# An issue-order mark on the VectorE modulations of a two-layer hybrid trunk

## The chip, the cores and the metric

The kernel runs on one NeuronCore of one Trainium2 chip. The metric is the device time of one execution in microseconds (us); lower is better. Three executions of the kernel before are given, and one more was taken with the hardware profiler; all rows below are from that one.

## The reference

The reference is one inference step of a diffusion trunk of two layers over 128 context tokens and 128 latent tokens, with a model width of 2048, in float32. What matters here, per layer:

```python
mods = silu(cond) @ w_mod[l] + b_mod[l]          # split in six: shift1, scale1, gate1, shift2, scale2, gate2
h = rms_norm(x, norm1_g) * (1 + scale1) + shift1
x = x + gate1 * (mixers(h @ w_in) @ w_out)       # linear attention, softmax attention, DeltaNet
h = rms_norm(x, norm2_g) * (1 + scale2) + shift2
x = x + gate2 * (square(relu(h @ w_ff1)) @ w_ff2)   # 4 * 2048 wide
```

The six modulations are numbered m = 0 to 5 in that order, so (0, 5) is gate2 of layer 0. Each is a product of two condition vectors with a 2048 x 2048 matrix.

## The kernel before, in words

Both groups of tokens go through the layers together: x lies as 16 tiles of 128 features by 256 tokens. Weights come from HBM in halves of 128x1024 float32 (512 KB, tile `raw`, six buffers, issued on SP's queue). For each half, ScalarE rounds it to `hi` and VectorE forms the rest `lo` = raw - hi (`split_half`), three buffers each; TensorE then does 16 matmuls with `hi` (the rounded activations and their rest) and 8 with `lo`. One half takes TensorE some 2.8 us in the profile. A unit of 128 output features has two halves and then an evacuation: `res_evac` for w_out and w_ff2 (VectorE adds gate times product to `x`; after w_out, and in the last pass of layer 0, it also scales the new x for the next norm into `hid` or `act` and adds its square to `sqacc`), `ff_evac` for w_ff1 (relu, square and rest).

The stretch that the change touches lies in each layer between w_out and w_ff1. w_out has 32 halves. Then `norm_lead` normalises: `get_rstd` sums the squares on TensorE (`st`), a Newton iteration of small VectorE instructions (`nv`, `n2t`, `n2y`) gives the reciprocal root, `diag` and a matmul (`bcb`) spread it. Meanwhile `lead_gemm` runs the first six units of w_ff1 (12 halves, tiles `gl`, `gl2`) on x scaled but not yet divided by the norm, and corrects them afterwards (`ld`). Interleaved with it `normed` makes the 16 tiles of the true normalised input: two `ht` on VectorE, two `hu` and one rounding on ScalarE, one rest (`act<-hu,act`) on VectorE, for each k. All later units of w_ff1 need all 16. The same function runs at the start of layer 1 on w_in, and in layer 1 again before w_ff1. Then follow four passes of w_ff1 and four of w_ff2, 32 halves each, in the order ff1(0), ff1(1), ff2(0), ff1(2), ff2(1), ff1(3), ff2(2), ff2(3).

The modulations are made in three ways. Two are made at the start. Most are made on TensorE (`mod_pe`: 16 steps, each with two w_mod halves and a few matmuls into `mod`). Four, listed in ONDV as (0, 5), (1, 1), (1, 0) and (1, 5), are made on VectorE by `mod_dv`: a transposed half `mraw` (512 KB, three buffers, SP's queue) is multiplied with a condition vector `sb` and summed along the row in one instruction (`tensor_tensor_reduce`; the profile calls it CUSTOM_DVE_ANT_0, with output `junk`, and a short accumulator read stands behind it; the order prints both as ISA). A modulation has 64 of these, 16 feature tiles by two conditions by two halves of the sum, so 256 in all. Below, such an instruction is a MAC. The first half of the sum goes to `part`, the second to `modc`. `junk` has one buffer, so the MACs of the program stay in sequence.

The order on each engine is not that of the code. The program is written down in one order and a scheduler (`schedule_with_timeline_sim=True`) then sets a static order per engine from its own model, with the written order as priority. `start_mod(l, 5)` is called in `ff1(0)`, behind `norm_lead`, but nothing holds its instructions there: they need only their own loads. They have to be done before `ff2(0)` uses gate2. An instruction that waits holds back all that stands behind it on its engine.

Of the kernel before, what the change touches and what calls it, by code (L numbers as in the profile page):

```python
# [10 lines left out]
F32 = mybir.dt.float32  # L11
# [4 lines left out]
ALU = mybir.AluOpType  # L16
# [25 lines left out]
def tile_hybrid_step(ctx: ExitStack, tc: tile.TileContext, A: dict, O: dict):  # L42
# [17 lines left out]
    ve, se = Timed(nc.vector, 1 / 960, 0.13), Timed(nc.scalar, 1 / 1400, 0.27)  # L60
# [339 lines left out]
    def mod_dv(l, m, modc, bm):  # L400
        mac = X["mac"]
        part = mdp.tile([P, 16, 2], F32, tag="part", name="part")
        i = ONDV.index((l, m))
        order = [(half, n) for half in range(2) for n in range(16)]

        def fetch(u):
            raw = mac.tile([P, 1024], F32, tag="mraw", name="mraw", bufs=3)
            nc.sync.dma_start(raw, A["w_modT"][i, order[u][0], order[u][1]])
            return raw

        nxt = fetch(0)
        for u, (half, n) in enumerate(order):
            raw = nxt
            if n == 0:
                sb = mac.tile([P, 2, 1024], F32, tag="sb", name="sb")
                nc.gpsimd.dma_start(sb.rearrange("p c j -> p (c j)"), scd[half].partition_broadcast(P))
                yield
            nxt = fetch(u + 1) if u + 1 < len(order) else None
            for c in range(2):
                junk = mac.tile([P, 1024], BF16, tag="junk", name="junk")  # L420
                ve.tensor_tensor_reduce(
                    out=junk, in0=raw, in1=sb[:, c], scale=1.0,
                    scalar=part[:, n, c : c + 1] if half else bm[:, m, n : n + 1], op0=ALU.mult, op1=ALU.add,
                    accum_out=modc[:, m, n, c : c + 1] if half else part[:, n, c : c + 1],
                )
            yield

    def mod_pe(l, m, modc, bm):
# [65 lines left out]
    def normed(rstd, dst, scl, shf):  # L494
        for k in range(16):
            t = X["np"].tile([P, 256], F32, tag="ht", name="ht", bufs=2)
            u = X["np"].tile([P, 256], F32, tag="hu", name="hu", bufs=2)
            for g in range(2):
                s = slice(g * P, g * P + P)
                ve.scalar_tensor_tensor(t[:, s], X["x"][:, k, s], scl[:, k, g : g + 1], rstd[:, s], ALU.mult, ALU.mult)  # L500
                se.activation(u[:, s], t[:, s], AF.Identity, bias=shf[:, k, g : g + 1])
            se.activation(dst[:, k, 0:256], u, AF.Copy)
            ve.tensor_tensor(dst[:, k, 256:512], u, dst[:, k, 0:256].bitcast(F32), ALU.subtract)
            yield

    def norm_lead(srcs, xsp, dst, scl, shf, ldp, sink=None):
        se.activation(xsp[:, :, 256:258], shf, AF.Copy)
        ve.tensor_tensor(xsp[:, :, 514:516], shf, xsp[:, :, 256:258].bitcast(F32), ALU.subtract)
        rstd = get_rstd()
        return lead_gemm(srcs, xsp, rstd, normed(rstd, dst, scl, shf), ldp, sink)  # L510
# [132 lines left out]
    for l in range(L):  # L643
# [171 lines left out]
        else:  # L815
            nlead = list(zip(FIRST, first))
            for j in FIRST[len(first) : 13]:
                for _ in range(2):
                    if nlead:
                        u, ps = nlead.pop(0)  # L820
# [832 lines left out]
```

## Time and profile before

| | us |
|---|---|
| median of three executions | 2579.03 |
| lowest and highest | 2578.31 and 2583.78 |
| the profiled execution, its own time | 2589.99 |
| span of its trace | 2588.2 |
| TensorE busy (matmuls) | 2503.7, 97% of the span |
| VectorE busy | 1822.5, 70% |
| ScalarE busy | 1225.7, 47% |

The profiled execution is 11 us above the median. Matmuls are pipelined and their ends are modelled, so a busy TensorE is not one at its peak. The same work appears once per layer, so a stretch of layer 0 can be held against its counterpart in layer 1.

### The profile page before, as it was taken

What the parts mean: (1) busy time and instruction counts of PE and PEld (TensorE: products, weight loads), DVE (VectorE), ACT (ScalarE), POOL (GpSimd) and SP (SyncE); (2) the same over time, 40 slices, a digit from 0 to 9 for tenths busy, and PEclk for the clock granted to TensorE, in tenths of its full rate; (3) what the DMA queues carried; (4) which work ended last, traced back from release to release, by engine and by line L of the source; (5) the groups of instructions that cost most, each with busy time, mean ns of one, the idle gap of its engine ahead of it and who ended that gap; (6) DMA issues with size and microseconds to landing.
All of it is one profiled execution on the core that took longest, in us unless ns stands there. A gap on an engine that the chain in (4) does not pass through costs nothing.

```text
span 2588.2 us, 47588 instructions
## 1 busy us (share of the span) xinstructions
PE 2503.7 (97%) x18860; PEld 2250.6 (87%) x18860; DVE 1822.5 (70%) x3510; ACT 1225.7 (47%) x1977; POOL 31.2 (1%) x59
## 2 busy tenths in 40 slices
PE   6999999988799999999999999999999999999999
PEld 4777677778799999999999888898999989999888
DVE  3456767698998889988456767697764565564665
ACT  3356244434655345344344763455575435445433
POOL 1000000000000000000000000000000000000000
PEclk9999999998899999999999999999999999999999
DMA  9875767797799999998777765445556666666664
GB/s 362 313 253 180 274 213 279 274 371 247 241 327 340 326 336 326 333 333 294 235 235 237 245 232 172 141 134 166 176 182 185 185 190 188 185 192 187 185 199 141
DMA packets 171935, 622.00 MB, mean 240 GB/s; under 512 B 20496, under 2 KB 21072, under 8 KB 170688
## 3 DMA queue, kind: packets, MB, share of 16 engines
q1 hardware_dynamic: 165600, 600.12, 68.4%
q0 software_dynamic: 3712, 15.59, 1.7%
q8 instruction: 148, 2.42, 0.4%
q10 hardware_dynamic: 2400, 3.24, 0.4%
q14 instruction: 75, 0.61, 0.1%
HBM read 612.57 MB, written 6.31 MB: 239 GB/s over the span
## 4 chain that ended last, share of the span: by engine, by line
PE 89%; DMA 4%; DVE 3%; ACT 2%; issue 1%; SPq 0%; ACTq 0%; DVEq 0%
PE g L86 67%; PE gt L86 6%; PE mod L86 4%; PE gl L86 4%; DMA raw<-w_mod 2%; DMA raw<-w_tok 1%; DVE lo L56 1%; ACT hi L56 1%; PE ga L86 1%; DVE junk L56 1%; PE eb L86 1%; DMA raw<-w_in 1%; PE fb L86 0%; PE fbm L86 0%; PE ob L86 0%
## 5 line engine op out<-in xcount | busy, mean ns | idle before, releaser
L56 ACT ACTIVATE hi<-raw 128x1024 fp32r<-128x1024 f32 (+1 forms) x742 | 784.5, 1058 | 1104.2 <-PE g L86 791.3
L56 DVE TENSOR_TENSOR lo<-raw,hi 128x1024 fp32r<-128x1024 f32 (+1 forms) x742 | 905.1, 1220 | 431.9 <-ACT hi L56 416.4
L86 PE MATMUL g<-act,hi 128*128 128x256 f32 (+1 forms) x7488 | 1054.1, 291 | 23.9 <-ACT ffr L56 7.4
L86 PEld LDWEIGHTS g<-act,hi 128*128 128x128 f32 x7488 | 955.6, 189 | 100.5 <-ACT hi L56 27.4
L86 PE MATMUL g<-act,lo 128*128 128x256 f32 x4000 | 562.8, 282 | 3.2 <-DVE lo L56 3.2
L86 PEld LDWEIGHTS g<-act,lo 128*128 128x128 f32 x4000 | 516.8, 190 | 14.5 <-DVE lo L56 4.9
L56 DVE SCALAR_TENSOR_TENSOR x<-g,modc,x 128x128 f32<-128x128 f32 x448 | 142.3, 348 | 185.8 <-PE g L86 180.5
L86 PE MATMUL g<-hid,hi 128*128 128x256 f32 (+1 forms) x1536 | 261.3, 319 | 0.0
L86 PEld LDWEIGHTS g<-hid,hi 128*128 128x128 f32 x1536 | 217.1, 188 | 23.1 <-ACT hi L56 5.0
L86 PE MATMUL mod<-raw,sc 128*32 128x512 f32 (+1 forms) x1280 | 152.1, 537 | 28.9 <-DMA raw<-w_mod 25.3
L56 DVE CUSTOM_DVE_ANT_0 junk<-mraw,sb,bm 128x1024 bf16<-128x1024 f32 x128 | 164.0, 1282 | 5.3 <-DMA sb<-scd 2.5
L56 DVE CUSTOM_DVE_ANT_0 junk<-mraw,sb,part 128x1024 bf16<-128x1024 f32 x128 | 164.1, 1282 | 2.1 <-DMA sb<-scd 1.7
L86 PE MATMUL gt<-hi,act 128*128 128x512 f32 x512 | 144.5, 414 | 3.7 <-ACT hi L56 3.7
L86 PE MATMUL g<-hid,lo 128*128 128x256 f32 x1024 | 141.8, 281 | 0.0
L86 PEld LDWEIGHTS g<-hid,lo 128*128 128x128 f32 x1024 | 134.6, 188 | 5.4
L86 PEld LDWEIGHTS gt<-hi,act 128*128 128x128 f32 x512 | 94.6, 192 | 41.1 <-issue 13.7
L86 PEld LDWEIGHTS mod<-raw,sc 128*32 128x32 f32 x1280 | 30.1, 110 | 67.0 <-DMA raw<-w_mod 21.6
L86 PE MATMUL gl<-hid,hi 128*128 128x258 f32 x384 | 74.8, 297 | 4.0 <-ACT hi L56 3.1
L86 PE MATMUL gt<-lo,act 128*128 128x512 f32 x256 | 75.7, 405 | 0.0
L86 PEld LDWEIGHTS gl<-hid,hi 128*128 128x128 f32 x384 | 62.9, 200 | 5.1 <-ACT hi L56 3.7
L86 PE MATMUL gl<-hid,lo 128*128 128x258 f32 x192 | 56.6, 296 | 3.6 <-DVE lo L56 3.6
L86 PEld LDWEIGHTS gt<-lo,act 128*128 128x128 f32 x256 | 48.3, 192 | 10.8 <-issue 0.4
(352 smaller groups left out, 1882.7 us busy)
## 6 DMA issues: line engine op xcount, KB each, us to landing
raw<-w_ff SPq DMA_DIRECT2D x512, 512.0 KB, 4.4
raw<-w_mod SPq DMA_DIRECT2D x256, 512.0 KB, 5.9
mraw<-w_modT SPq DMA_DIRECT2D x128, 512.0 KB, 6.0
raw<-w_in SPq DMA_DIRECT2D x86, 512.0 KB, 4.4
raw<-w_tok SPq DMA_DIRECT2D x64, 512.0 KB, 4.5
raw<-w_out SPq DMA_DIRECT2D x64, 512.0 KB, 4.4
sb<-scd POOLq DMA_DIRECT2D x8, 1024.0 KB, 8.7
raw<-w_in SPq DMA_DIRECT2D x16, 448.0 KB, 6.2
```

The lines of the kernel that those rows point to most:

```text
L56: return f(out, *a, **kw)
L86: i = nc.tensor.matmul(out, lhsT=lhsT, rhs=rhs, start=start, stop=stop, **kw)
```

## The change

The change stamps two instructions with one mark, "normed". Instructions of one engine that carry the same mark keep the order in which the program writes them down; the scheduler may not swap them. No instruction is added or removed.

```diff
@@ mod_dv
             for c in range(2):
                 junk = mac.tile([P, 1024], BF16, tag="junk", name="junk")
-                ve.tensor_tensor_reduce(
+                i_ = ve.tensor_tensor_reduce(
...
                 )
+                if u == 0 and c == 0:
+                    tc.stamp_issue_order_token(i_.ins, "normed")
             yield
@@ normed
             se.activation(dst[:, k, 0:256], u, AF.Copy)
-            ve.tensor_tensor(dst[:, k, 256:512], u, dst[:, k, 0:256].bitcast(F32), ALU.subtract)
+            i = ve.tensor_tensor(dst[:, k, 256:512], u, dst[:, k, 0:256].bitcast(F32), ALU.subtract)
+            if k == 15:
+                tc.stamp_issue_order_token(i.ins, "normed")
             yield
```

So the first MAC of each of the four VectorE modulations, and with it the rest of that modulation, stays behind the last instruction of every `normed` that is written before it. What the scheduler makes of this is shown at three places of VectorE's order.

**VectorE, w_out of layer 0** (x, hid and sqacc are the evacuation of a unit, lo the rest of a weight half, ISA junk a MAC). Before:

```order
L56 ISA junk,part<-mraw,sb,bm 128x1024
L56 ISA part 128x1
L56 SCALAR_TENSOR_TENSOR x<-g,modc,x 128x128 x2
L56 ISA junk,part<-mraw,sb,bm 128x1024
L56 ISA part 128x1
L56 SCALAR_TENSOR_TENSOR hid<-x,s_147,hid 128x128 x2
L56 TENSOR_TENSOR sqacc<-sqacc,sqt 128x256
```

With the change, from the same place:

```order
L56 SCALAR_TENSOR_TENSOR x<-g,modc,x 128x128 x2
L56 SCALAR_TENSOR_TENSOR hid<-x,s_147,hid 128x128 x2
L56 TENSOR_TENSOR sqacc<-sqacc,sqt 128x256
L56 TENSOR_TENSOR lo<-raw,hi 128x1024
L56 SCALAR_TENSOR_TENSOR x<-g,modc,x 128x128 x2
```

Every MAC has left this stretch, 32 of them; nothing else is added to it.

**VectorE, the Newton iteration of the norm in layer 0** (nv, n2t, n2y). Before:

```order
L56 ISA junk,modc<-mraw,sb,part 128x1024
L56 ISA modc 128x1
L56 TENSOR_SCALAR nv<-st 128x2
L56 TENSOR_TENSOR lo<-raw,hi 128x1024
L56 ISA junk,modc<-mraw,sb,part 128x1024
L56 ISA modc 128x1
L56 TENSOR_SCALAR n2t<-nv 128x2
L56 ISA junk,modc<-mraw,sb,part 128x1024
L56 ISA modc 128x1
L56 TENSOR_SCALAR n2y<-n2t 128x2
```

With the change:

```order
L56 TENSOR_TENSOR lo<-raw,hi 128x1024
L56 TENSOR_SCALAR nv<-st 128x2
L56 TENSOR_SCALAR n2t<-nv 128x2
L56 TENSOR_SCALAR n2y<-n2t 128x2
L56 SCALAR_TENSOR_TENSOR n2t<-nv,n2y 128x2
L56 TENSOR_TENSOR n2t<-n2t,n2y 128x2
L56 SCALAR_TENSOR_TENSOR n2y<-n2t,n2y 128x2
```

Before, a MAC stood between nearly every two steps of the iteration; now the steps follow each other. The first MAC of the program now stands right behind the last `act<-hu,act` of this norm.

**VectorE, the last pass of w_ff2 in layer 0, ff2(3)**. Before:

```order
L56 TENSOR_TENSOR lo<-raw,hi 128x1024
L56 SCALAR_TENSOR_TENSOR x<-g,modc,x 128x128 x2
L56 TENSOR_TENSOR lo<-raw,hi 128x1024
L56 SCALAR_TENSOR_TENSOR act<-x,s_6811,act 128x128 x2
L56 TENSOR_TENSOR lo<-raw,hi 128x1024
```

With the change:

```order
L56 TENSOR_TENSOR lo<-raw,hi 128x1024
L56 ISA junk,modc<-mraw,sb,part 128x1024
L56 ISA modc 128x1
L56 SCALAR_TENSOR_TENSOR x<-g,modc,x 128x128 x2
L56 TENSOR_TENSOR lo<-raw,hi 128x1024
L56 ISA junk,modc<-mraw,sb,part 128x1024
L56 ISA modc 128x1
L56 SCALAR_TENSOR_TENSOR act<-x,s_6811,act 128x128 x2
L56 TENSOR_TENSOR lo<-raw,hi 128x1024
```

The 256 MACs have moved back as one train: before, the last of them stood at the start of ff2(2) and ff2(3) had none; now ff2(2) holds 34 and ff2(3) 28, about one per half, and one more stands behind them. TensorE's own order changes only by a few positions of `mod` and `gl` matmuls.

## Rows read from the trace of the kernel before

**Rows 1.** Busy time, share of the span and instructions of two engines.

```profile
PE 2503.7 (97%) x18860; PEld 2250.6 (87%) x18860; DVE 1822.5 (70%) x3510; ACT 1225.7 (47%) x1977; POOL 31.2 (1%) x59
```

**Rows 2.** Costliest groups: busy us, mean ns | idle before, releaser. MACs, lo.

```profile
L56 DVE TENSOR_TENSOR lo<-raw,hi 128x1024 fp32r<-128x1024 f32 (+1 forms) x742 | 905.1, 1220 | 431.9 <-ACT hi L56 416.4
...
L56 DVE CUSTOM_DVE_ANT_0 junk<-mraw,sb,bm 128x1024 bf16<-128x1024 f32 x128 | 164.0, 1282 | 5.3 <-DMA sb<-scd 2.5
```

**Rows 3.** Stretches: length, busy of PE, PEld, DVE, ACT, POOL; PEclk, DMA share, GB/s.

```profile
506.40:566.10 59.70, 52.68 (x404) 43.73 (x405) 52.72 (x96) 21.27 (x39) 0.00 (x0) 0.97 0.98 386
...
606.20:692.80 86.60, 66.19 (x424) 61.35 (x423) 80.14 (x161) 46.95 (x112) 0.53 (x1) 0.80 0.67 225
740.00:1200.00 460.00, 460.00 (x3857) 438.57 (x3856) 417.48 (x598) 207.05 (x287) 2.65 (x5) 1.00 0.92 333
1215.00:1410.00 195.00, 195.00 (x1637) 186.25 (x1636) 109.06 (x176) 85.05 (x116) 0.00 (x0) 1.00 0.72 228
1778.70:1858.00 79.30, 79.29 (x672) 79.30 (x673) 53.88 (x100) 43.95 (x73) 0.00 (x0) 1.00 0.63 198
1858.00:1911.90 53.90, 50.24 (x416) 49.78 (x415) 43.40 (x97) 44.79 (x112) 0.00 (x0) 1.00 0.54 175
1890.00:1912.00 22.00, 19.37 (x163) 19.17 (x162) 16.26 (x30) 21.32 (x58) 0.00 (x0) 1.00 0.56 187
```

**Rows 4.** The MACs alone by stretch: DVE busy; PEclk, DMA share, GB/s.

```profile
506.40:606.20 99.80, 41.07 (x32) 0.98 0.95 355
606.20:692.80 86.60, 41.23 (x32) 0.80 0.67 225
740.00:1200.00 460.00, 214.65 (x168) 1.00 0.92 333
```

**Rows 5.** PE in order of time at five places: start us, us, what.

```profile
506.37 2.54 PE L86 MATMUL g<-act,hi 128*128 128x256 f32 x16 [2.14 <-DVE x L56]
...
606.17 0.40 PE L86 MATMUL gl<-hid,hi 128*128 128x258 f32 x2
...
692.83 2.06 PE L86 MATMUL g<-act,hi 128*128 128x256 f32 x16
...
1858.03 0.40 PE L86 MATMUL gl<-hid,hi 128*128 128x258 f32 x2
...
1911.90 2.06 PE L86 MATMUL g<-act,hi 128*128 128x256 f32 x16
```

**Rows 6.** The mod tile's instructions, 506.3 to 606.2: busy of PE, PEld, DVE, ACT.

```profile
506.30:606.20 99.90, 9.48 (x72) 2.24 (x72) 0.19 (x1) 0.57 (x1) 0.98 0.95 355
```

**Rows 7.** PE groups, 506.4 to 606.2.

```profile
L86 PE MATMUL g<-act,hi 128*128 128x256 f32 x448 | 59.1, 285 | 6.0 <-ACT hi L56 3.8 <-DVE x L56 2.1
L86 PE MATMUL g<-act,lo 128*128 128x256 f32 x224 | 32.4, 288 | 3.2 <-DVE lo L56 3.2
```

**Rows 8.** PE groups, 606.2 to 692.8.

```profile
L86 PE MATMUL gl<-hid,hi 128*128 128x258 f32 x192 | 39.6, 308 | 3.0 <-ACT hi L56 2.1 <-ACT ldc L56 0.9
L86 PE MATMUL gl<-hid,lo 128*128 128x258 f32 x96 | 29.7, 309 | 3.6 <-DVE lo L56 3.6
L86 PE MATMUL g<-act,hi 128*128 128x256 f32 x80 | 16.3, 358 | 11.3 <-DVE act L56 6.0 <-ACT ffr L56 4.8 <-ACT hi L56 0.6
...
L86 PE MATMUL mod<-raw,sc 128*32 128x512 f32 x8 | 1.9, 1061 | 2.6 <-DMA raw<-w_mod 2.6
```

**Rows 9.** The same for layer 1, 1858 to 1911.9.

```profile
L86 PE MATMUL g<-act,hi 128*128 128x256 f32 x80 | 10.4, 282 | 2.6 <-ACT ffr L56 2.6
```

**Rows 10.** DVE in order of time: first and last step of both Newton iterations.

```profile
612.75 0.16 DVE L56 TENSOR_SCALAR nv<-st 128x2 f32<-128x2 f32 x1
...
635.64 0.42 DVE L56 TENSOR_TENSOR diag<-c_ident,n2y 128x256 f32<-128x256 f32 x1
...
1863.89 0.16 DVE L56 TENSOR_SCALAR nv<-st 128x2 f32<-128x2 f32 x1 [0.51 <-PE st L86]
...
1867.62 0.42 DVE L56 TENSOR_TENSOR diag<-c_ident,n2y 128x256 f32<-128x256 f32 x1
```

## The prediction

> **What bounds the kernel now.** The first view is the busy time by engine [rows 1]: TensorE is busy for 97% of the span, VectorE for 70%. So TensorE sets the end, and a change of VectorE's order pays only where TensorE waits or runs slowly. The costliest groups [rows 2] say what VectorE spends: 742 `lo` of 1.22 us and the MACs of 1.28 us each, of which one of the two forms is listed (128 of 256).
>
> The second view is the table of stretches [rows 3]. Between 740 and 1200 us TensorE is busy for 460 of 460 us, although VectorE carries 168 MACs there [rows 4] and is itself busy for 417.48, or 91%. A MAC beside w_ff1 and w_ff2 thus costs TensorE nothing. The other 64, those of (0, 5), stand 32 in w_out and 32 in the norm with its lead [rows 4], and those are the two stretches of layer 0 where TensorE does not keep up: 52.68 of 59.70 us, then 66.19 of 86.60 at a granted clock of 0.80 [rows 3], that is 0.80 of 2.4 GHz.
>
> Third, TensorE in order of time [rows 5] gives the boundaries, and so the price by comparison with layer 1, which does the same work without MACs. w_out takes 99.8 us in layer 0 (506.37 to 606.17) and 79.3 in layer 1 (the row of that length in rows 3, which ends where layer 1's `gl` begin). From the first `gl` to the first `g` after the lead it is 86.7 us (606.17 to 692.83) against 53.9 (1858.03 to 1911.90).
>
> **The change, part by part.** Nothing is added or removed. All 256 MACs go back by 64 places of their train: (0, 5) starts behind the norm, where (1, 1) stood, and so on, and the last 62 or so come to lie beside ff2(2) and ff2(3), which had one between them. Three terms follow.
>
> *w_out of layer 0, 32 MACs leave.* Of the 20.5 us more than in layer 1, 9.5 are `mod` steps on TensorE, which stay (72 matmuls, 9.48 us [rows 6]). The rest, 11.0 us, is the upper bound. The groups of this stretch [rows 7] name 3.8 us of waiting for `hi` and 3.2 for `lo`; the 2.1 behind `x` are the start of w_out, not a MAC. The `lo` wait is VectorE's own queue. The `hi` wait is ScalarE's, which is busy for only 21.27 of 59.70 us, while the DMA engines stand at a share of 0.98 and 386 GB/s [rows 3]: `hi` is late because `raw` is. Sixteen `mraw` loads of 512 KB (a load feeds two MACs), 8.4 MB, leave this stretch with the MACs, except the first three, which SP still issues early; so I count this wait as gone too. Lower bound 3.2, upper 11.0, taken: 3.8 + 3.2 = **7.0**, the two waits that rows name.
>
> *Norm and lead of layer 0, 32 MACs leave.* The difference to layer 1 is 86.7 - 53.9 = 32.8 us; eight `mod` matmuls stay, 8/72 of 9.48 or 1.1, which leaves 31.7. It can be built up a second way. TensorE's waits [rows 8] are 3.0 + 3.6 + 11.3 + 2.6 = 20.5 us, against 2.6 in layer 1 [rows 9], so 17.9. Its matmuls take 308, 309 and 358 ns where layer 1's take 282 [rows 9]: 192 x 26 + 96 x 27 + 80 x 76 ns = 13.7 us. Together 31.6. The origin is the Newton iteration: 612.75 to 635.64 in layer 0, 22.9 us, and 1863.89 to 1867.62 in layer 1, 3.7 us [rows 10]; a MAC between nearly every two steps puts 1.28 us into a chain of 0.16 us steps, everything behind it (16 `normed` tiles, the six corrections) is 19 us later, and the first `g` waits 6.0 for `act`. With the waits gone I expect a granted clock of 1.00, as layer 1 has it.
>
> Not all of it is got back. In the new order six MACs stand in the last halves of this stretch, 6 x 1.28 = 7.7 us. In the corresponding 22 us of layer 1 VectorE is busy for 16.26, so 5.7 are free, but ScalarE is full (21.32) [rows 3] and TensorE waits 2.6 for `ffr` [rows 9], so some of the MACs delay something: between 0 and 7.7. I take 3, since 7.7 - 5.7 = 2.0 don't fit and the order is fixed. Bounds 24.0 and 31.7, taken **28.7**.
>
> *ff2(2) and ff2(3), 62 MACs arrive.* In 1215 to 1410 us VectorE is busy for 109.06 of 195 us [rows 3]. With 63 x 1.28 = 80.6 more, one from the edge included, it is 189.7, or 97%. The densest stretch known to do no harm is 91% [rows 3]. If VectorE could not be packed closer than that, the stretch would take 189.7/0.91 = 208.5 us, a loss of 13; if it can, 0. The row at 91% shows no wait of TensorE at all, and `lo` has three buffers to even out a late one, so I stay nearer to zero: a loss of **3**. What (1, 1), (1, 0) and (1, 5) feed lies in layer 1, where TensorE's order stays as it was; (0, 5) is needed at ff2(0), and at about 1.15 MACs per half its 64 end there in time. DMA is no bound in the new place (share 0.72, 228 GB/s), and SP's queue has the same loads in a later place.
>
> The sum is 7.0 + 28.7 - 3.0 = 32.7 us: the profiled execution would go from 2590.0 to 2557.3, and the median, which lies 11 us under that execution, from 2579.0 to **2546**. With all bounds at their worst (3.2 + 24.0 - 13 = 14.2) it is 2565, at their best (11.0 + 31.7 = 42.7) 2536.
>
> **Rivals.** *Only VectorE's own waits go.* If the DMA queue keeps `hi` late and the clock stays low for its own reason, the gain is what rows put down to VectorE: 3.2 [rows 7], 3.6 and 6.0 [rows 8], 12.8 us: 2566. Against it: layer 1 has the clock at 1.00 in the same stretch.
>
> *It comes to nothing.* The MACs of ff2(3), where each unit has the longer evacuation, 28 in number, go on the path whole: 28 x 1.28 = 36 us, more or less the gain, about 2580. This is also where it ends if the first three loads or the new order of `mraw` keep TensorE waiting as long as before.
>
> *VectorE becomes the bound at the new place, and the kernel is slower.* At 97% every MAC that stands ahead of a late `lo` or of an evacuation delays TensorE, and what is lost in ff2(2) is not made up in ff2(3). All 64 displaced MACs on the path cost 82 us: 2579 - 35.7 + 82 = 2625. It turns to a loss when more than 35.7/1.28 = 28 of the 64 stand in front of something that TensorE waits for. For it: 189.7 of 195. Against it: 740 to 1200. The Trainium skill (Perfetto Trace Analysis, Optimization Strategy) says that where the busiest engine changes from one regime to the next, interleaving the regimes may help; the change takes VectorE's MACs out of one regime and crowds them into another, which by that rule loses their cover. The trace agrees with the rule's premise, not for the place left, but for the new one at most.
>
> **How the numbers follow.** A difference of 0.2%, 5 us, is about what a measurement of this kernel can tell from no change. Forecast 0.80; only VectorE's waits 0.10; nothing 0.05; slower 0.05. The first two are both faster: 0.90. The range goes from the best bound of the forecast, 2536, to the first rival, 2566, and holds 0.9; the forecast's own worst, 2565, lies inside.
>
> **What would show it.** Right: no MAC before the norm's end; `nv` to `diag` in about 4 us in layer 0 also; first `gl` to first `g` in about 58 us at a granted clock of 1.00; w_out in about 93 us with the DMA share below 0.98; TensorE nearly unbroken in ff2(2) and ff2(3) with VectorE at about 97%. Wrong: a wait of TensorE for `lo` or `x` of over 10 us in ff2(2) and ff2(3); a clock still at 0.80 in the lead although the iteration is short; a new wait of the first `g` for `act` or `ffr` behind the six MACs; a wait of ff2(0)'s `x` for `modc`.

## The result and the profile after

| | before | with the change |
|---|---|---|
| median, us | 2578.67 | 2550.19 |
| lowest and highest, us | 2578.04 and 2583.78 | 2542.92 and 2557.12 |
| the profiled execution, us | 2589.99 | 2542.92 |

The ratio is 0.9885 with an interval of 0.9854 to 0.9915: 28.5 us faster. The forecast was 2546, the range 2536 to 2566. The two profiled executions lie on opposite sides of their medians: the one of before is 11 us above its own, slower than all four timed executions, and this one is 7 us below, the fastest of its four. Their difference of 47 us therefore has to be read stretch by stretch.

The page of the kernel after, busy time by engine: VectorE does the same work (1822.5 us before [rows 1]), TensorE is busy for 22 us less, with as many matmuls.

```profile
PE 2481.6 (98%) x18860; PEld 2237.1 (88%) x18860; DVE 1822.1 (72%) x3510; ACT 1223.3 (48%) x1977; POOL 31.1 (1%) x59
```

The stretches that answer to [rows 3]: the first 59.7 us of w_out, then from the first `gl` to the sixth half of `g` behind the lead (what the prediction calls the first `g` after the lead; five halves of `g` lie inside, in every run alike), then ff2(2) and ff2(3). Columns: length, busy time of PE, PEld, DVE, ACT, POOL, granted clock, DMA share, GB/s.

```profile
493.40:553.10 59.70, 57.76 (x469) 49.57 (x470) 32.10 (x62) 26.48 (x48) 0.00 (x0) 1.00 0.96 357
585.60:641.20 55.60, 51.21 (x424) 49.92 (x423) 49.15 (x108) 44.98 (x112) 0.00 (x0) 1.00 0.57 178
1160.00:1355.00 195.00, 195.00 (x1619) 185.27 (x1618) 179.07 (x295) 84.01 (x115) 0.53 (x1) 1.00 0.88 314
```

VectorE has lost 21 us in the first row and 31 in the second, and gained 70 in the third; TensorE has no gap in the third. VectorE's share in the third is 92% (179.07 of 195), where 97% was forecast. The bounds in TensorE's order of time answer to [rows 5]:

```profile
493.40 2.11 PE L86 MATMUL g<-act,hi 128*128 128x256 f32 x16 [2.14 <-DVE x L56]
...
585.56 0.40 PE L86 MATMUL gl<-hid,hi 128*128 128x258 f32 x2
...
637.27 1.07 PE L86 MATMUL mod<-raw,sc 128*32 128x512 f32 x8 [3.36 <-DMA raw<-w_mod]
638.27 2.16 PE L86 MATMUL g<-act,hi 128*128 128x256 f32 x16
...
641.21 2.05 PE L86 MATMUL g<-act,hi 128*128 128x256 f32 x16
```

w_out takes 585.56 - 493.40 = 92.2 us (99.8 before), norm and lead 641.21 - 585.56 = 55.7 (86.7). VectorE's iteration takes 3.7 us instead of 22.9 [rows 10], and the first and last MAC of the kernel are where the order put them:

```profile
591.42 0.16 DVE L56 TENSOR_SCALAR nv<-st 128x2 f32<-128x2 f32 x1 [0.51 <-PE st L86]
...
595.15 0.42 DVE L56 TENSOR_TENSOR diag<-c_ident,n2y 128x256 f32<-128x256 f32 x1
...
627.94 1.28 DVE L56 CUSTOM_DVE_ANT_0 junk<-mraw,sb,bm 128x1024 bf16<-128x1024 f32 x1
...
1359.72 1.28 DVE L56 CUSTOM_DVE_ANT_0 junk<-mraw,sb,part 128x1024 bf16<-128x1024 f32 x1
```

TensorE's groups in the norm and lead answer to [rows 8]: no wait for `lo`, `act` or `ffr` is left, and the matmuls are back from 308, 309 and 358 ns.

```profile
L86 PE MATMUL gl<-hid,hi 128*128 128x258 f32 x192 | 35.2, 286 | 1.0 <-ACT hi L56 1.0
L86 PE MATMUL gl<-hid,lo 128*128 128x258 f32 x96 | 26.9, 282 | 0.0
L86 PE MATMUL g<-act,hi 128*128 128x256 f32 x80 | 10.4, 283 | 0.0
...
L86 PE MATMUL mod<-raw,sc 128*32 128x512 f32 x8 | 1.1, 605 | 3.4 <-DMA raw<-w_mod 3.4
```

So 7.6 + 31.0 us come from the two stretches. What follows the sixth half, 1895.4 us before, takes 1899.9, a loss of 4.5. Net 34.1; the other 13.0 us between the two profiles lie ahead of w_out (506.37 against 493.40), a part of the program that the change does not touch.

### The profile page after: what moved, and what is told of

Read it like the earlier page. It is cut to its first block, busy times and chain, and to the rows that moved or that the text cites. A ratio compares the mean times of both kernels' runs of the same rounds, so it can differ in the third digit from the quotient of the medians.

```text
span 2541.1 us, 47597 instructions
## 1 busy us (share of the span) xinstructions
PE 2481.6 (98%) x18860; PEld 2237.1 (88%) x18860; DVE 1822.1 (72%) x3510; ACT 1223.3 (48%) x1977; POOL 31.1 (1%) x59
## 4 chain that ended last, share of the span: by engine, by line
PE 90%; DMA 5%; ACT 2%; DVE 2%; issue 0%; SPq 0%; ACTq 0%; DVEq 0%
PE g L86 68%; PE gt L86 6%; PE mod L86 4%; PE gl L86 4%; DMA raw<-w_tok 1%; DMA raw<-w_out 1%; ACT hi L56 1%; DMA raw<-w_mod 1%; PE ga L86 1%; PE fbm L86 1%; PE fb L86 1%; DVE lo L56 1%; PE eb L86 1%; DMA raw<-w_in 1%; DMA x<-xT 0%; PE oatb L86 0%
## 5 line engine op out<-in xcount | busy, mean ns | idle before, releaser
L86 PEld LDWEIGHTS mod<-raw,sc 128*32 128x32 f32 x1280 | 31.0, 109 | 59.7 <-DMA raw<-w_mod 13.7
L86 PE MATMUL gl<-hid,lo 128*128 128x258 f32 x192 | 53.9, 282 | 0.0
```

The source lines that it names most:

```text
L86: i = nc.tensor.matmul(out, lhsT=lhsT, rhs=rhs, start=start, stop=stop, **kw)
```

## The experiments

All times in this table are from one profile each, in us; the median is that of all runs of the kernel. The kernel before had medians of 2578.67, 2582.01 (E1 to E4), 2579.02 (E5 to E8) and 2579.68 (E9 to E12).

| kernel | median | w_out starts | w_out | `nv` to `diag` | first `gl` to sixth `g` | sixth `g` to layer 1's first `gl` | rest |
|---|---|---|---|---|---|---|---|
| before | 2578.67 | 506.4 | 99.8 | 22.9 | 86.7 | 717.6 | 1177.8 |
| change | 2550.19 | 493.4 | 92.2 | 3.7 | 55.7 | 721.1 | 1178.8 |
| E1 mark on the 33rd MAC | 2556.58 | 496.9 | 98.6 | 5.1 | 61.3 | 717.6 | 1180.7 |
| E2 only the iteration kept free | 2566.91 | 499.0 | 100.2 | 5.1 | 69.5 | 717.9 | 1180.0 |
| E3 without (1, 5) | 2544.37 | 499.2 | 92.5 | 3.7 | 57.1 | 717.9 | 1178.1 |
| E4 (1, 5) in layer 1 | 2546.83 | 498.1 | 92.1 | 3.7 | 58.3 | 717.6 | 1181.6 |
| E5 only w_out kept free | 2573.84 | 498.9 | 93.0 | 21.9 | 85.1 | 717.6 | 1180.7 |
| E6 32 MACs, one load | 2552.00 | 495.7 | 93.3 | 3.6 | 62.8 | 717.7 | 1181.5 |
| E7 16 MACs, 16 loads | 2554.04 | 497.6 | 101.3 | 3.7 | 56.6 | 717.9 | 1179.5 |
| E8 64 MACs more | 2622.89 | 496.4 | 91.5 | 3.7 | 55.0 | 720.2 | 1255.8 |
| E9 the change again | 2549.46 | 497.8 | 90.6 | 3.7 | 58.5 | 721.1 | 1183.1 |
| E10 E4 again | 2547.70 | 498.7 | 92.5 | 3.7 | 58.2 | 717.6 | 1182.6 |
| E11 mark behind the lead | 2546.74 | 494.1 | 90.8 | 3.7 | 53.9 | 718.8 | 1184.6 |
| E12 E4 and E11 | 2548.77 | 498.0 | 91.8 | 3.7 | 53.9 | 717.6 | 1185.1 |

The theory was the one of the prediction: MACs delay TensorE in w_out by their loads and their place in VectorE's queue, in the norm by standing in the iteration, and cost little elsewhere. The rivals are named with each run.

### Are the two terms separate? E1 and E5

E1 marks the 33rd MAC of (0, 5); E5 keeps the mark on the first, but holds it behind the last evacuation of w_out.

```diff
@@ E1, mod_dv
-                if u == 0 and c == 0:
+                if u == (16 if i == 0 else 0) and c == 0:
@@ E5, res_evac (and no mark in normed)
-                        ve.scalar_tensor_tensor(
+                        i = ve.scalar_tensor_tensor(
...
+                    if m == 2 and n == 15:
+                        tc.stamp_issue_order_token(i.ins, "normed")
```

E1: 

> The mark of (0, 5) is put on its 33rd MAC instead of its first, so 32 MACs stay beside w_out and only the 32 of the norm and lead move. If the gain is a sum of separate terms, w_out of layer 0 is back at 99 to 100 us (99.8 before, 92.2 with the change), the stretch from the first gl to the sixth g is about 56 us (86.7 and 55.7), and what follows it takes about 2 us more than before instead of 4.5: some 29 us under the kernel before and 5 over the change. Rival: if the loads for the MACs beside w_out are what delays the norm, the stretch stays above 65 us although no MAC stands in it.

E5: 

> The mark is put on the last evacuation of w_out instead of the last normed tile: the MACs leave w_out, but the first 32 or so of the train stand in the norm and the lead, a MAC again between nearly every two steps of the Newton iteration. If the terms are separate, w_out of layer 0 takes 92 to 93 us (99.8 before), nv to diag some 20 us again, the stretch from the first gl to the sixth g 84 to 90 us, and the run is some 7 us under the kernel before. Rival: if the loads beside w_out had made the norm slow (late raw halves), the stretch falls under 75 us although the MACs are in it.

Measured: E1 0.9901 (0.9886 to 0.9915), E5 0.9970 (0.9957 to 0.9983). Where the MACs stay, the old time stays: w_out 98.6 in E1, the norm 85.1 in E5. Where they go, it falls: 61.3 and 93.0. The terms are separate, and the norm's is the larger, by nearly four times (25.4 against 6.8 us). The medians agree: E1 gains 25.4 us, E5 5.2, and their sum, 30.6, is close to the 28.5 and 30.2 of the change's two measurements. E1's 61.3 is 5 us more than I expected, though only seven MACs stand there; TensorE's one large wait in it is 5.6 us for `ffr`. VectorE is not full in this stretch, 50.81 of 61.30 us:

```profile
595.40:656.70 61.30, 53.61 (x424) 51.95 (x423) 50.81 (x110) 45.67 (x112) 0.00 (x0) 0.94 0.63 205
```

### Is it the iteration? E2

```diff
@@ E2: E1, and the mark taken from normed and put on diag, in bcast_cols
-        ve.tensor_tensor(d, bc1(ident, n), bc(rs, P), ALU.mult)
+        i = ve.tensor_tensor(d, bc1(ident, n), bc(rs, P), ALU.mult)
+        if tag == "ht":
+            tc.stamp_issue_order_token(i.ins, "normed")
```

> The same, but the 33rd MAC of (0, 5) is held only behind diag, the last step of the Newton iteration, and not behind the 16 normed tiles: 17 MACs stand in the stretch again, none of them inside the iteration. If the iteration is the origin of the long norm, nv to diag takes 4 to 5 us and the stretch 56 to 64 us. Rival, that a MAC costs its 1.28 us wherever it stands between w_out and w_ff1: 17 of them leave the stretch at 56 + 22 = 78 us or more, at a granted clock below 0.95.

Measured: 0.9943 (0.9928 to 0.9957). The iteration is short, 5.1 us, and the stretch still takes 69.5: between the two expectations, so the theory holds in part only. The stretch and its MACs alone (DVE), then TensorE's groups in it:

```profile
599.20:668.60 69.40, 56.91 (x424) 53.67 (x423) 65.91 (x137) 47.06 (x112) 0.00 (x0) 0.90 0.71 227
...
599.20:668.60 69.40, 25.48 (x20) 0.90 0.71 227
```

```profile
L86 PE MATMUL g<-act,hi 128*128 128x256 f32 x80 | 15.2, 348 | 8.6 <-ACT ffr L56 4.7 <-DVE act L56 3.3 <-ACT hi L56 0.6
L86 PE MATMUL mod<-raw,sc 128*32 128x512 f32 x8 | 1.9, 1062 | 2.1 <-DMA raw<-w_mod 2.1
```

VectorE is busy for 65.91 of 69.40 us, 95%; before it was 80.14 of 86.60, 93% [rows 3]. Set beside E11, which has 2 MACs and 53.9 us, E2's 18 more cost 15.6 us, 0.87 each, and the 30 more of before cost 32.8, 1.09 each. So in E2 a MAC costs most of its 1.28 us although it stands outside the iteration. VectorE's sum gives a floor: with the work that the order puts there, the stretch cannot fall below 65.91 us in E2 and 80.14 before, whatever the iteration does. That accounts for 12.0 of E2's 15.6 us and for 26.2 of the 32.8 before. What the iteration adds of its own is not shown, since E2 also has 12 MACs fewer than before. Nor is the sum all: in E1 VectorE is busy for only 83%, and 5 MACs more than E11's two cost 7.4 us, 1.5 each, through the wait for `ffr`.

### What costs in w_out, MACs or loads? E6 and E7

Both are E1 with one thing less beside w_out.

```diff
@@ E6: one load for the first half of (0, 5)
-            nxt = fetch(u + 1) if u + 1 < len(order) else None
+            if not (i == 0 and u < 15):
+                nxt = fetch(u + 1) if u + 1 < len(order) else None
@@ E7: one MAC for each of these loads
-            for c in range(2):
+            for c in range(1 if i == 0 and half == 0 else 2):
```

E6: 

> The arrangement of the run with the mark on the 33rd MAC (w_out 98.55 us with 32 MACs and 16 loads beside it), but all 32 MACs of the first half read one loaded tile, so 15 loads of 512 KB are left out, and modulation (0, 5) is wrong in value; 27 of the MACs stay beside w_out, 5 stand behind it. If the wait for hi comes from loads that share the DMA engines, w_out falls by 3 to 4 us, to about 95, and 3 us of waiting for lo are left. Rival: it is all VectorE's queue, and w_out stays at 98; or all DMA, and it is 92.

E7: 

> The counterpart: the same arrangement with all 16 loads beside w_out, but one MAC for each instead of two, so the second condition vector of (0, 5) is left out in the first half of the sum. If VectorE's queue is behind the wait for lo, w_out falls by 2 to 3 us from 98.55, to about 96. Rivals: the loads alone matter, and it stays at 98; the MACs alone, and it is at 93 to 95.

Measured: E6 93.3, E7 101.3. TensorE's groups in w_out, of E1, then E6, then E7:

```profile
L86 PE MATMUL g<-act,hi 128*128 128x256 f32 x448 | 58.3, 282 | 5.9 <-ACT hi L56 3.7 <-DVE x L56 2.1
L86 PE MATMUL g<-act,lo 128*128 128x256 f32 x224 | 31.6, 283 | 3.6 <-DVE lo L56 3.6
```

```profile
L86 PE MATMUL g<-act,hi 128*128 128x256 f32 x448 | 58.1, 282 | 2.9 <-DVE x L56 2.1 <-ACT hi L56 0.8
L86 PE MATMUL g<-act,lo 128*128 128x256 f32 x224 | 31.5, 283 | 1.1 <-DVE lo L56 1.1
```

```profile
L86 PE MATMUL g<-act,hi 128*128 128x256 f32 x448 | 60.7, 289 | 10.2 <-ACT hi L56 8.1 <-DVE x L56 2.1
L86 PE MATMUL g<-act,lo 128*128 128x256 f32 x224 | 31.6, 285 | 0.0
```

The loads decide. With 29 MACs and without the 15 loads the waits for `hi` and `lo` fall from 7.3 to 1.9 us, and w_out is about where the change has it. With half the MACs and all loads the wait for `lo` goes, but the one for `hi` grows by more, to 8.1, and w_out is no shorter. So the wait for `lo` that the profile put down to VectorE was late `raw` for the most part. MACs as such cost some 1 to 3 us beside w_out (E6's 93.3 against 90.6 to 92.5 without any). That E7 is above E1 is not all its doing: E2, with E1's order in w_out, takes 100.2 us at a granted clock of 0.97, which is E7's, where E1 had 1.00. In E7 a `mraw` buffer is free sooner and the loads come sooner (the last MAC starts 71 us into w_out, in E1 90); a w_out half lands in 8.1 us (median), in 6.2 in E1 and 5.2 in E6. The DMA share of the first 59.7 us is 1.02 in both E1 and E7.

### The six MACs at the end of the lead. E11 and E12

The mark is moved to the last evacuation of the lead; E12 also has (1, 5) in layer 1, as E4 below.

```diff
@@ E11, ff_evac (the mark in normed stays; the later one decides)
-                ve.tensor_tensor(hid[:, j, 256:512], r2, hid[:, j, 0:256].bitcast(F32), ALU.subtract)
+                i = ve.tensor_tensor(hid[:, j, 256:512], r2, hid[:, j, 0:256].bitcast(F32), ALU.subtract)
+                if hid is act and j == 5:
+                    tc.stamp_issue_order_token(i.ins, "normed")
```

E11: 

> The change, with the mark on the last evacuation of the lead instead of the last normed tile: the six MACs leave the last halves of the stretch from the first gl to the sixth g. If they cost 3 us there, as predicted, it falls to 52 to 53 us; if the wait of a mod step for its w_mod half (3.3 us at that place in the change) covers them, it stays at 55 to 58. The train ends about 8 MACs later, beside the first steps of the first norm of layer 1, which by the run with the doubled MACs should cost up to 10 us: 2550 to 2560. Rival: those 8 cost nothing, since only two stand inside the iteration.

E12: 

> The mark on the last evacuation of the lead, and (1, 5) in layer 1: no MAC in the norm and lead of layer 0, none in ff2(3), none in a norm of layer 1. By the terms it equals the run with (1, 5) in layer 1 within 1 us, or is up to 3 us faster if the six MACs had a price.

Measured: 0.9870 (0.9854 to 0.9885) and 0.9873 (0.9858 to 0.9888). The stretch is 53.9 us in both, layer 1's value, against 55.0 to 58.5 in the seven profiles with the change's order there (change, E3, E4, E7 to E10): the six cost 1 to 4.6 us. The lower figure belongs to a granted clock of 1.00 (change and E8, 55.7 and 55.0), the upper one to 0.94 (E4, E9 and E10, 58.2 to 58.5). The rival, that the `mod` step's wait covers them, falls: that wait shrinks with them. First E9, which is the change, then E11:

```profile
588.40:646.90 58.50, 54.10 (x425) 51.98 (x424) 49.93 (x109) 45.32 (x112) 0.00 (x0) 0.94 0.58 184
...
640.10 1.93 PE L86 MATMUL mod<-raw,sc 128*32 128x512 f32 x8 [3.36 <-DMA raw<-w_mod]
```

```profile
585.00:638.90 53.90, 51.34 (x425) 49.98 (x424) 44.52 (x100) 44.79 (x112) 0.00 (x0) 1.00 0.60 178
...
634.43 1.07 PE L86 MATMUL mod<-raw,sc 128*32 128x512 f32 x8 [1.12 <-DMA raw<-w_mod]
```

Neither median tells these two from the change, and their profiles show where the gain goes. E11's train ends later, beside layer 1's first norm. TensorE's first `gl` there, then VectorE's first step of the iteration, the last MAC and `diag`:

```profile
1357.68 0.41 PE L86 MATMUL gl<-act,hi 128*128 128x258 f32 x2
...
1368.19 0.15 DVE L56 TENSOR_SCALAR nv<-st 128x2 f32<-128x2 f32 x1
...
1371.12 1.29 DVE L56 CUSTOM_DVE_ANT_0 junk<-mraw,sb,part 128x1024 bf16<-128x1024 f32 x1
...
1374.29 0.42 DVE L56 TENSOR_TENSOR diag<-c_ident,n2y 128x256 f32<-128x256 f32 x1
```

`nv` comes 10.5 us behind that `gl`, against 7.3 in the change and 5.8 before. From this `gl` to the first one of layer 1's second norm E11 takes 454.4 us, the change 447.1 and E9 450.1. So the tail costs some 4 to 7 us, and the rival that it costs nothing falls. E12 has no such tail (448.6), but its 64 MACs in layer 1 make TensorE wait for `x` behind the second norm, for 4.2 us where E4 waits 1.3 and the change not at all. E12, then E4:

```profile
PE g L86 <- DVE x L56: 4.2, 2, 2.4
```

```profile
PE g L86 <- DVE x L56: 1.3, 1, 1.3
```

### The end of the train. E3, E4 and E10

E3 leaves (1, 5) out, so that gate2 of layer 1 is zero; E4 and E10 (the same kernel twice) start it in layer 1.

```diff
@@ E3, start_mod
+            if (l, m) == (1, 5):
+                nc.gpsimd.memset(modc[:, m], 0.0)
+                yield
+                return
@@ E4 and E10
-FF0M = (1, 0, 5, 2, 4, 3)
+FF0M = (1, 0, 2, 4, 3)
...
-        rate[:] = [R3, 0 if last else V3]
+        rate[:] = [R3, V3]
```

E3: 

> The change, without the 64 MACs and the loads of modulation (1, 5), which is set to zero: gate2 of layer 1 is left out. The train then ends ahead of ff2(2), as it did before. If the 4.5 us that the change loses behind the lead come from VectorE being crowded in ff2(2) and ff2(3), the time from the sixth g to the end goes from 1899.9 back to 1895 or a little under. Rival: it stays near 1900, and the loss comes from elsewhere or is the spread between executions.

E4: 

> The change, with (1, 5) written down in layer 1 behind its second norm, where its gate is used: its 64 MACs lie beside w_ff1 of layer 1. VectorE is busy there for about two thirds of the time and the DMA engines for 0.54 to 0.63. If those have room, this equals the run without (1, 5): about 1895 us from the sixth g to the end, 4 to 5 us faster than the change. Rival: the MACs cost in layer 1 what they save in layer 0, and it equals the change.

E10: 

> The change with (1, 5) beside w_ff1 of layer 1, again, against the change on the same chip. ff2(3) of layer 0 without its 28 MACs gains 3.5 us, some 2.5 us of new waits for x stood in w_ff1 and w_ff2 of layer 1: 1 to 4 us faster than the change, an interval that may hold zero.

Measured: 0.9850 (0.9833 to 0.9866), 0.9860 (0.9845 to 0.9876) and 0.9869 (0.9848 to 0.9890). From the sixth `g` to layer 1 all three are back at 717.6 to 717.9, before's value, and E3 takes 1896.0 to the end, as the theory had it; so the 3.5 us come with the last 64 MACs. But TensorE waits nowhere in ff2(2) or ff2(3), 195.00 of 195.00 us. Its order of time shows what it does instead; the `mod` steps beside ff2(3) of before, then of after (three of many in each):

```profile
1304.48 1.06 PE L86 MATMUL mod<-raw,sc 128*32 128x512 f32 x8
1325.50 1.06 PE L86 MATMUL mod<-raw,sc 128*32 128x512 f32 x8
1346.54 1.07 PE L86 MATMUL mod<-raw,sc 128*32 128x512 f32 x8
```

```profile
1292.09 1.05 PE L86 MATMUL mod<-raw,sc 128*32 128x512 f32 x4
1296.10 1.05 PE L86 MATMUL mod<-raw,sc 128*32 128x512 f32 x4
1323.68 1.05 PE L86 MATMUL mod<-raw,sc 128*32 128x512 f32 x2
1336.20 1.06 PE L86 MATMUL mod<-raw,sc 128*32 128x512 f32 x6
1356.29 1.05 PE L86 MATMUL mod<-raw,sc 128*32 128x512 f32 x4
1358.42 1.05 PE L86 MATMUL mod<-raw,sc 128*32 128x512 f32 x4
```

Three steps of eight matmuls are torn in two, and a piece of two, four or six takes 1.05 us as the whole does: 3 x 1.06 = 3.2 of the 3.5 us. The orders bear it out: before, E1, E3, E4 and E10 have only whole groups there; the change has three torn ones and takes 721.1 in both profiles; E11's order tears one and takes 718.8, E8's tears two and takes 720.2. E4 and E10 then lose some of it again in layer 1 (2.7 us of waits for `x` in E4 where E3 has 1.7), and E10 against E9, on the same chip, is 1.8 us faster with intervals that overlap almost wholly. A version that clearly beats the change was not found.

### When the train runs into the next norm. E8

```diff
@@ E8, mod_dv
-            for c in range(2):
+            for c in (0, 1, 0, 1) if i == 3 else range(2):
```

> The change, with every MAC of (1, 5) issued twice, so that 64 more run through the end of the train. The order keeps about one per half in ff2(2) and ff2(3) and puts the 64 that are left into the first norm of layer 1, between the steps of its Newton iteration and its normed tiles. If the price of a MAC is set by the place where it stands, ff2(2) and ff2(3) stay as in the change, and layer 1's first norm and lead lose 35 to 82 us: 2585 to 2632, no faster than the kernel before and probably slower. Rival: if a norm can carry MACs at the cost of the cover only, as an engine that is two thirds busy would, it loses under 20 us.

Measured: 1.0164 (1.0139 to 1.0188), 2622.89 us, 73 more than the change. ff2(2) and ff2(3) again have no gap; layer 1's first norm and lead bear it all. Stretches, then TensorE's waits from 1363 to 1480 us:

```profile
1160.00:1363.00 203.00, 203.00 (x1685) 192.32 (x1685) 187.46 (x310) 87.11 (x120) 0.53 (x1) 1.00 0.81 278
1363.00:1500.00 137.00, 67.34 (x494) 61.07 (x493) 127.69 (x244) 51.68 (x114) 1.07 (x2) 0.73 0.51 167
```

```profile
PE g L86 <- DVE ld L56: 57.3, 1, 57.3
PE bcb L86 <- DVE diag L56: 5.0, 1, 5.0
```

That is the slower rival of the prediction at another place: not ff2, where the order itself never puts more than about one MAC to a half (VectorE 187.46 of 203 us, 92%), but the norm behind it. TensorE's loss there is mainly one wait of 57.3 us for `ld`, on a VectorE that is busy for 127.69 of 137 us. The change's train ends 10 us ahead of that norm's first step (the last MAC at 1359.72, `nv` at 1369.65).

### The spread. E9

The kernel is that of the change.

> The change itself once more, with five rounds and a second profile, since its executions lay between 2543 and 2557 us. If the stretches ahead of w_out, where every engine's order is that of before, only spread between executions, w_out starts at 493 to 500 us as in all runs since, the stretch from the first gl to the sixth g is 55 to 58 us, the rest 1900 us, and the median is 28 to 35 us under the kernel before. Rival: the start of w_out is at 506 as in the profile of before, and the gain is larger than the two stretches explain.

Measured: 2549.46 us, 0.9873 (0.9853 to 0.9892). In the thirteen profiles other than that of before w_out starts at 493 to 499 us, E1 and E2 included, which have their MACs beside it. So before's 506.4 goes with an execution 11 us above its median rather than with the MACs; a second profile of the kernel before was not taken. Behind layer 1's first `gl` the change took 1178.8 us in one profile and 1183.1 in the other; that is the spread in which the small terms go under.

## Why the prediction was right, point by point

**The sum.** Forecast 32.7 us; measured 28.5 and, in E9, 30.2. The two large terms were right in size and place; part of their reasons was not, as the terms show. The change's profile gives 34.1 behind the start of w_out, E9's 9.2 + 28.2 - 3.5 - 5.3 = 28.6. The difference between the two is layer 1's spread and the clock in the lead.

**w_out, 7.0 taken.** Measured 7.6 (7.3 to 9.2 in the seven other profiles with its order there: E3, E4, E8 to E12). At a granted clock of 1.00 on both sides, E1's 98.6 against 90.6 to 92.2 (change, E8, E9, E11, E12), it is 6.4 to 8.0. The `hi` part was right in its reason. The step "the `lo` wait is VectorE's own queue" failed: E6 keeps the MACs and the wait falls from 3.6 to 1.1 us. Right size, half of it for the wrong reason, and to that extent luck.

**Norm and lead, 28.7 taken.** Measured 31.0 in the change's profile, 28.2 in E9's. The subtraction against layer 1 was right to about 1 us: E11 reaches 53.9 us, what layer 1 takes, with its `mod` step included, for which the sum left 1.1. The six MACs were put at 3 and cost 1 to 4.6. The step that failed is "the origin is the Newton iteration": E2 frees it, with 20 of the 32 MACs left, and keeps 15.6 of the 32.8 us. The row that says so stood in [rows 3], VectorE 80.14 of 86.60, 93% in the one stretch where TensorE was at 66.19; I read the chain and left the sum out. The size of the term does not hang on this step, since it was taken from the difference between the layers. The second way of adding it up reads layer 1 from its `g` group alone; the `gl` of that stretch wait 1.0 for `hi` and take 285 ns, and 42 `lo` matmuls of `g` at 354 ns instead of 280 are not in it. With these it gives 33 us, still near 31.7.

```profile
L86 PE MATMUL gl<-hid,hi 128*128 128x258 f32 x192 | 35.1, 285 | 1.0 <-ACT hi L56 1.0
```

The Trainium skill (Perfetto Trace Analysis, Identifying the Most-Contended Engine) takes VectorE's busy share as a fair measure of how near it is to its limit. E2's 95% and E5's 80.39 of 85.10 us agree; E1's 83% shows a stretch that is made longer by a wait and not by the sum.

**ff2(2) and ff2(3), 3 taken.** Measured 3.5, and not VectorE's crowding, which was the reason given: it is busy for 179.07 of 195 us there and TensorE has no wait. It is for the most part three torn `mod` steps in TensorE's order, which the text ahead of the prediction mentions as a few positions and the sum costed at nothing. E1, with 31 MACs in ff2(2), loses nothing there. The right size was luck. VectorE's 97% did not come about either: the 63 MACs were there, with 80.6 us as summed, but all of VectorE's work was 179.07 us and not 189.7, so what happens at 97% no run shows.

**The clock.** 1.00 was forecast in the lead; the change's profile and E8's have 1.00, E3 and E7 0.97, E4, E9 and E10 0.94, with the same order there. So the forecast holds in some executions only.

**The rivals.** Only VectorE's waits (2566): excluded, the matmuls' own time came back. Nothing (2580): excluded. Slower by the new place: no sign of it in ff2, but E8 shows the mechanism, at 64 MACs more and in the next norm. The prediction held against the change there the rule of the Trainium skill that interleaving regimes may help (Perfetto Trace Analysis, Optimization Strategy). The trace agrees with it for w_ff1 and w_ff2 of layer 0, where 168 MACs leave TensorE busy for 460 of 460 us [rows 3]; beside the norm, where each cost 0.87 to 1.5 us, interleaving did not help.

## What to carry to other kernels

Work for a second engine is free or dear by its place, and the price of a place is read by subtracting a stretch with it from the same stretch without it, as layers repeat; that number was right here even where its explanation was not. In such a stretch look at the busy time of the engine that carries the work before looking for a chain: the stretch cannot be shorter than that sum, 80.14 of 86.60 us here, wherever the work stands. Where the sum leaves room, as in E1 (50.81 of 61.30), the place still sets the price. When a fixed order moves a train of work back, ask where its tail lands and which groups on the bounding engine it tears.

## What the runs showed that was not expected

A `mod` step's matmuls take 1.05 us as a run of two, four or six, and 1.06 as a run of eight; each split of a run added about 1 us to the stretch.

Fewer MACs did not make w_out shorter: 101.3 us in E7 with 16 and 16 loads, against 98.6 to 100.2 in E1, E2 and before with 32 and the same loads. That loads which find their buffer free sooner crowd out the weights fits E7's longer landing (8.1 us against 6.2 in E1), but was not tested by itself.

The same wait in the lead, 3.2 to 3.4 us for a `w_mod` half in the same order, is followed by matmuls at full pace in the change's profile (the step's 605 ns, granted clock of the stretch 1.00) and by slower ones in E3 (946 ns, 0.97), E4, E9 and E10 (1060 ns, 0.94); between 1.00 and 0.94 the stretch is 2.6 to 2.8 us longer. What decides between them the runs do not show.
